# HGRN2 weights in blocks of 32 tokens: products on the four 32-column quarters of the array, and the level of 32 tokens as a product of its own

## The chip, the cores and the metric

The kernel runs on one core of a Trainium2 chip. A core has five engines that run side by side, each with its own stream of instructions: TensorE (PE, matrix products from SBUF into PSUM; a weight load, PEld, stands before every product), VectorE (DVE), ScalarE (ACT), GpSimd (POOL) and SyncE (SP, which starts transfers). They wait for one another by semaphores. The metric is the device time of one execution in microseconds (us).

## The reference, cut to what matters

Two layers over 256 tokens and a residual of width 2048. Each layer normalises the residual, projects it, runs two kinds of heads on the result (gated DeltaNet, 8 heads, and HGRN2, 8 heads, all of width 128), projects back, and adds a gated embedding. The change touches the HGRN2 heads alone, which compute

```
k = (1 - lb) * sigmoid(-f);  log_f = log(lb + (1 - lb) * sigmoid(f));  G = cumsum(log_f)
rel = masked_exp(causal, G[r] - G[s])           # for every channel d, for s <= r
A[r, s] = sum_d q[r, d] * k[s, d] * rel[r, s, d]
o[r] = (q[r] * exp(G[r])) @ S + sum_s A[r, s] * v[s]
```

`rel` differs from channel to channel, so A is not one plain product of a q matrix and a k matrix.

## The kernel before

The work of a layer is a long run of dense products (the projections "in", "out", "gate", "up"), all issued by `run_step`. Weights come from HBM in pieces (`load`, queued on SP), are split by ACT into `whi` (L398) and by DVE into the rest `wlo` (L400), and PE multiplies `whi`, `wlo` and the activations' two parts, 128x512 a time. PE's instructions stay in the order in which the program calls them (`PEOrder`, all at L334; transposes at L337). The other engines' instructions are put in order by the framework's scheduler.

The heads' work is laid between these products. Heads go in four groups of two (g = 0 to 3; `hg02` is layer 0, group 2; `dn02` the DeltaNet heads of that group). A group's mixer is a generator: after each `yield n` it goes on when n more steps of dense products have been issued (`tick`); the tables `DELAY` and `DELAY_AT` hold these n. So a mixer's small products stand in PE's order as short blocks between dense products.

The HGRN2 mixer is `HG.q_side`. Channels lie on the 128 partitions; the columns hold four pieces i (two heads x two chunks of 128 tokens). A is made by levels. At the level of unit u the tokens are taken in pairs of neighbouring runs of u tokens; s lies in the first run, r in the second, and with G's value at the end of the first run, `rel` is a factor of s times a factor of r. `factors(us)` builds for each u a tile X with k[s] exp(end - G[s]) in the first runs and q[r] exp(G[r] - end) in the second (DVE at L960, L962, L967, L974, exponentials on ACT at L965). `products` multiplies X by its own second runs:

```
for b in (0, 64):
    xb = x[:, i, b:b + 64]
    PE.matmul(pa[b:b + 64, c:c + 32], xb,
              xb.rearrange("p (n a b) -> p n a b", a=2, b=u)[:, :, 1], start=True, stop=True)
```

A product has 64 tokens as stationary columns and writes to PSUM partitions 0 to 63 or 64 to 127: one half of the array's columns. `place` copies the pairs that belong to the level by a mask `ms` from PSUM into `Ad` (128 x 4 x 64), on DVE, L991. Units 1 to 32 fill a block of 64 tokens; unit 64 and unit 128 are products of their own, copied by ACT. The level of single tokens and the diagonal share a product of 96 columns with `q8` (64 columns of q, 32 of q times a factor).

PE so has four blocks a group: first, the diagonal with level 1, then level 2 (bank "1"); second, levels 4 and 8; third, levels 16 and 32; fourth, levels 64 and 128. After the fourth, ACT copies `Ad`'s two halves into the block diagonal of `hA` (L1035), the 64 x 64 block (L1036) and `hAx`, and `po` multiplies them by v. With two layers and four groups there are eight such groups. A product of fp32 operands appears in the trace as two records, so that the program's x8 is x16 there; a product of two fp32r operands and a transpose are one.

Of the kernel before, what the change touches and what calls it, by code (L numbers as in the profile page):

```python
# [8 lines left out]
F32 = mybir.dt.float32  # L9
# [3 lines left out]
ALU = mybir.AluOpType  # L13
# [125 lines left out]


NPAR = _lay_params()
UNITS = (1, 2, 4, 8, 16, 32)


NMASK = 32 + 32 * len(UNITS)


def const_arrays():
    i = np.arange(128)
    c = np.zeros((128, 4 * 128 + 256 + 64), np.float32)  # L150
    c[:, 0:128] = np.eye(128)
    c[:, 128:256] = 1.0
    c[:, 256:384] = i[:, None] > i[None, :]
    c[:, 384:512] = i[:, None] <= i[None, :]
    c[:, 512:768] = (np.arange(256) % 128 != 0)[None, :]
    c[:, 768:832] = i[:, None] % 64 == np.arange(64)[None, :]
    s, r = i[:, None], i[None, :]
    m = np.zeros((128, NMASK), np.int32)
    m[:, 0:32] = (s % 64 // 32 == np.arange(32)[None, :] // 16) & (s % 32 < 16)
    for n, u in enumerate(UNITS):  # L160
        low = (s % 64 // (2 * u) == np.arange(32)[None, :] // u) & (s % (2 * u) < u)
        m[:, 32 + 32 * n:64 + 32 * n] = low
    return c, m


# [1 line left out]
def trunk(ctx: ExitStack, tc: tile.TileContext, head, xT, x, pT, W, par, fw, cst, msk, eye, out):  # L167
    nc = tc.nc
    pool = lambda name, bufs, **kw: ctx.enter_context(tc.tile_pool(name=name, bufs=bufs, **kw))
    cp = pool("const", 1)  # L170
# [10 lines left out]
    V, S, G = nc.vector, nc.scalar, nc.gpsimd  # L181
# [2 lines left out]

    h = [hp.tile([128, 2, 512], F32, name=f"h{c}") for c in range(4)]
    pr = cp.tile([128, NPAR], F32, name="pr")
    cs = cp.tile([128, 832], F32, name="cs")
    ms = cp.tile([128, NMASK], I32, name="ms")

    def first(out, in_):  # L190
# [77 lines left out]
        return [tuple(t) for t in a]  # L268

    ident, ones, SL, UI = (cs[:, 128 * j:128 * j + 128] for j in range(4))  # L270
    keep, ident64 = cs[:, 512:768], cs[:, 768:832]
    epsc = cp.tile([128, 1], F32, name="epsc")
    G.memset(epsc, EPS)
    lnhd = cp.tile([128, 1], F32, name="lnhd")
# [10 lines left out]
    hA = cp.tile([128, 4, 128], F32, name="hA")  # L285

    def clear_scratch():
        V.tensor_copy(SLr, SL)
        G.memset(hA[64:128, :, 0:64], 0.0)
        zero = tp.tile([128, 512], F32, tag="tmp", name="zero")  # L290
        G.memset(zero, 0.0)
        tc.keep_in_program_order(nc.scalar.dma_start(out=dfull(d2), in_=zero.rearrange("p (i c) -> p i c", i=4)))
# [8 lines left out]
    def bc1(ap, n):  # L301
        return ap.unsqueeze(1).to_broadcast([ap.shape[0], n, ap.shape[1]])
# [36 lines left out]
    PE = PEOrder()  # L339
# [222 lines left out]
    def mix(tag, n, bufs, name):  # L562
        return mp.tile([128, n], F32, tag=tag, name=name, bufs=bufs)
# [324 lines left out]
    class HG:  # L888
# [12 lines left out]
        def hi(self, ps, c0):  # L901
            self.v = mix("iv", 512, 2, self.n + "iv")
            for t in range(2):
                S.activation(self.v[:, 256 * t:256 * t + 256], ps[t][:, c0:c0 + 256], AF.Copy, scale=self.row.rt[:, t:t + 1])
            self.done.add("i")
            yield 1
# [24 lines left out]
        def q_side(self, qr):  # L931
            l, g, n = self.l, self.g, self.n

            q8 = mix("hq", 768, 1, n + "q").rearrange("p (a c) -> p a c", c=96)
            q = q8[:, :, 0:64]
            sg = tmp(n + "qsg")
            sigmoid(sg, qr)
            c64 = lambda ap: ap.rearrange("p (a c) -> p a c", c=64)
            V.tensor_tensor(q, c64(qr), c64(sg), ALU.mult)
            yield self.after("f")  # L940
            k, Gc = self.k, self.G
            k4 = v4(k)

            lo = lambda ap, u: ap.rearrange("p (n a b) -> p n a b", a=2, b=u)[:, :, 0]
            hi = lambda ap, u: ap.rearrange("p (n a b) -> p n a b", a=2, b=u)[:, :, 1]

            def hq(u):

                if u < 64:
                    return q.rearrange("p a (n c b) -> p a n c b", c=2, b=u)[:, :, :, 1]  # L950
                return q.rearrange("p (n c a) b -> p n c a b", c=2, a=u // 64)[:, :, 1]

            def factors(us):


                X = mix("hX", 1024, 2, n + f"X{us[0]}")[:, :512 * len(us)]
                xs = [X[:, 512 * j:512 * j + 512] for j in range(len(us))]
                for u, x in zip(us, xs):
                    ends = lo(Gc, u)[:, :, u - 1:u].to_broadcast([128, 256 // u, u])
                    V.tensor_tensor(lo(x, u), ends, lo(Gc, u), ALU.subtract)  # L960
                    if u < 128:
                        V.tensor_tensor(hi(x, u), hi(Gc, u), ends, ALU.subtract)  # L962
                    else:
                        V.tensor_copy(hi(x, u), hi(Gc, u))
                S.activation(X, X, AF.Exp)  # L965
                for u, x in zip(us, xs):
                    V.tensor_tensor(lo(x, u), lo(x, u), lo(k, u), ALU.mult)  # L967
                    hx = hi(x, u)
                    if u < 64:
                        hx = hx.rearrange("p (a n) b -> p a n b", a=8)  # L970
                    elif u == 128:
                        hx = hx.rearrange("p n (a b) -> p n a b", b=64)
                    hx_q = hq(u) if u != 64 else hq(u)[:, :, 0]
                    V.tensor_tensor(hx, hx, hx_q, ALU.mult)  # L974
                return [v4(x) for x in xs]

            def products(us, xs, pa, o=0):

                for j, (u, x) in enumerate(zip(us, xs)):
                    for i in range(4):  # L980
                        for b in (0, 64):
                            xb = x[:, i, b:b + 64]
                            c = o + 128 * j + 32 * i
                            PE.matmul(pa[b:b + 64, c:c + 32], xb,
                                      xb.rearrange("p (n a b) -> p n a b", a=2, b=u)[:, :, 1], start=True, stop=True)

            def place(us, ws):
                for u, w in zip(us, ws):
                    mo = 32 + 32 * UNITS.index(u)
                    mk = ms[:, mo:mo + 32].rearrange("p (n b) -> p n b", b=u)  # L990
                    V.copy_predicated(Ad.rearrange("p i (n a b) -> p i n a b", a=2, b=u)[:, :, :, 1],  # L991
                                      mk.unsqueeze(1).to_broadcast([128, 4, 32 // u, u]),
                                      w.rearrange("p i (n b) -> p i n b", b=u))

            bank = lambda x: pm.tile([128, 512], F32, tag="m", name=n + "pa" + x)
            v32 = lambda ap: ap.rearrange("p (i c) -> p i c", c=32)
            if self.wait("q"):
                yield self.wait("q")
            x1 = q8[:, :, 64:96]
            c32 = lambda ap: ap.rearrange("p (a n) b -> p a (n b)", a=8)  # L1000
            V.tensor_tensor(x1, c32(hi(Gc, 1)), c32(lo(Gc, 1)), ALU.subtract)
            S.activation(x1, x1, AF.Exp)
            V.tensor_tensor(x1, x1, hq(1)[:, :, :, 0], ALU.mult)
            xs = factors((2,))
            yield self.wait("a")

            Ad = mix("hAd", 256, 1, n + "Ad").rearrange("p (i c) -> p i c", i=4)
            pa = bank("1")
            for i in range(4):
                for b in (0, 64):  # L1010
                    PE.matmul(pa[b:b + 64, 96 * i:96 * i + 96], k4[:, i, b:b + 64], q8[:, 2 * i + b // 64, :],
                              start=True, stop=True)
            nxt = factors((4, 8))
            products((2,), xs, pa, 384)
            w1 = pa[:, :384].rearrange("p (i c) -> p i c", c=96)
            V.tensor_tensor(Ad, w1[:, :, 0:64], bc1(ident64, 4), ALU.mult)
            place((1, 2), (w1[:, :, 64:96], v32(pa[:, 384:512])))
            yield self.wait("u1")
            for us, then in (((4, 8), (16, 32)), ((16, 32), (64, 128))):
                xs, nxt = nxt, factors(then)  # L1020
                pa = bank(f"{us[0]}")
                products(us, xs, pa)
                place(us, (v32(pa[:, 0:128]), v32(pa[:, 128:256])))
                yield self.wait(f"u{us[0]}")
            xs = nxt
            pa = bank("64")
            for i in range(4):
                PE.matmul(pa[0:64, 64 * i:64 * i + 64], xs[0][:, i, 0:64], xs[0][:, i, 64:128], start=True, stop=True)

            for hh in range(2):  # L1030
                PE.matmul(pa[:, 256 + 128 * hh:384 + 128 * hh], xs[1][:, 2 * hh], xs[1][:, 2 * hh + 1],
                          start=True, stop=True)
            A = hA
            for b in (0, 64):
                S.copy(A[b:b + 64, :, b:b + 64], Ad[b:b + 64])  # L1035
            S.copy(A[0:64, :, 64:128], pa[0:64, :256].rearrange("p (a b) -> p a b", b=64))  # L1036
            Ax = v4(mix("hAx", 256, 1, n + "Ax"))
            S.copy(Ax, v4(pa)[:, 2:4])
# [153 lines left out]
    for l in range(DEPTH):  # L1192
# [24 lines left out]
        for c, k4 in order:  # L1217
# [6 lines left out]
            for q in range(0, 4, w):  # L1224
# [19 lines left out]
                s = run_step(ps[c], act)  # L1244
# [27 lines left out]
        for c, k4 in order:  # L1272
# [15 lines left out]
            if end and k4[3] == KT - 9:  # L1288

                n = state["next"]  # L1290
# [46 lines left out]
```

## Time and profile before

| | |
|---|---|
| median of the runs shown | 1275.14 us (three runs: 1274.43, 1275.14, and one of 6480.21) |
| profiled execution | 1273.78 us, of which 1272.1 us from the first to the last instruction |
| PE products, weight loads | 1259.3 us (99%), 1048.7 us (82%), 7297 records each |
| DVE, ACT, POOL busy | 926.7 us (73%), 782.6 us (62%), 64.4 us (5%) |
| granted TensorE clock | 0.998 |
| DMA | 220.87 MB, mean 174 GB/s |

PE's records overlap: a dense product lasts 0.39 us but the next starts 0.23 us after it. So for PE the distance from start to start is the cost, and the busy time only says that there is hardly a hole.

### The profile page before, as it was taken

What the parts mean: (1) busy time and instruction counts of PE and PEld (TensorE: products, weight loads), DVE (VectorE), ACT (ScalarE), POOL (GpSimd) and SP (SyncE); (2) the same over time, 40 slices, a digit from 0 to 9 for tenths busy, and PEclk for the clock granted to TensorE, in tenths of its full rate; (3) what the DMA queues carried; (4) which work ended last, traced back from release to release, by engine and by line L of the source; (5) the groups of instructions that cost most, each with busy time, mean ns of one, the idle gap of its engine ahead of it and who ended that gap; (6) DMA issues with size and microseconds to landing.
All of it is one profiled execution on the core that took longest, in us unless ns stands there. A gap on an engine that the chain in (4) does not pass through costs nothing.

```text
span 1272.1 us, 19685 instructions
## 1 busy us (share of the span) xinstructions
PE 1259.3 (99%) x7297; PEld 1048.7 (82%) x7297; DVE 926.7 (73%) x1744; ACT 782.6 (62%) x1395; POOL 64.4 (5%) x55
## 2 busy tenths in 40 slices
PE   9999999999999999999999999999999999999996
PEld 8988888888888888888888888888888888888886
DVE  7789689787796855547668886897777968555476
ACT  7666666666666654447557667667665766444464
POOL 0100010020000000000002000100100000000010
PEclk9999999999999999999999999999999999999999
DMA  8665545455554455555555555544555545555563
GB/s 286 192 229 159 172 159 165 131 166 178 167 167 153 144 174 182 183 189 191 184 185 169 176 163 159 170 141 135 178 182 170 162 150 171 182 182 185 183 198 132
DMA packets 78239, 220.87 MB, mean 174 GB/s; under 512 B 15552, under 2 KB 25280, under 8 KB 78144
## 3 DMA queue, kind: packets, MB, share of 16 engines
q1 hardware_dynamic: 59040, 211.73, 50.7%
q10 hardware_dynamic: 19104, 7.90, 2.3%
q8 instruction: 57, 0.93, 0.3%
q14 instruction: 38, 0.31, 0.1%
HBM read 214.88 MB, written 4.72 MB: 173 GB/s over the span
## 4 chain that ended last, share of the span: by engine, by line
PE 93%; DVE 5%; DMA 1%; issue 1%; ACT 1%; SPq 0%; DVEq 0%; ACTq 0%
PE out L334 14%; PE gate L334 13%; PE in1dk L334 7%; PE in0dk L334 7%; PE in1hf L334 6%; PE in0hf L334 6%; PE in0dv L334 6%; PE in1dv L334 6%; PE in0hi L334 5%; PE in1hi L334 5%; PE up L334 2%; DVE wlo L400 1%; PE in1dz L334 1%; PE in0dz L334 1%; PE gaterun L334 0%
## 5 line engine op out<-in xcount | busy, mean ns | idle before, releaser
L400 DVE TENSOR_TENSOR wlo<-raw,whi 128x1024 fp32r<-128x1024 f32 (+1 forms) x392 | 480.3, 1228 | 248.7 <-ACT whi L398 247.0
L398 ACT ACTIVATE whi<-raw 128x1024 fp32r<-128x1024 f32 (+1 forms) x392 | 411.4, 1051 | 352.1 <-PE out L334 88.3
L334 PE MATMUL in1hf<-whi,n1hi 128*128 128x512 f32 x128 | 52.5, 410 | 0.0
L334 PE MATMUL in1hi<-whi,n1hi 128*128 128x512 f32 x128 | 51.6, 403 | 0.0
L334 PE MATMUL in1dk<-whi,n1hi 128*128 128x512 f32 x128 | 51.2, 400 | 0.0
L334 PE MATMUL in1dk<-wlo,n1hi 128*128 128x512 f32 x128 | 50.0, 391 | 0.2 <-DVE wlo L400 0.2
L334 PE MATMUL gate<-whi,g0hi 128*128 128x512 f32 x128 | 50.2, 392 | 0.0
L334 PE MATMUL in1hf<-whi,n1lo 128*128 128x512 f32 x128 | 50.1, 391 | 0.0
L334 PE MATMUL in1hi<-whi,n1lo 128*128 128x512 f32 x128 | 50.0, 391 | 0.0
L334 PE MATMUL in1hf<-wlo,n1hi 128*128 128x512 f32 x128 | 49.9, 390 | 0.0
L334 PE MATMUL in1dk<-whi,n1lo 128*128 128x512 f32 x128 | 49.9, 390 | 0.0
L334 PE MATMUL in1hi<-wlo,n1hi 128*128 128x512 f32 x128 | 49.9, 390 | 0.0
L334 PE MATMUL gate<-whi,g0lo 128*128 128x512 f32 x128 | 49.8, 389 | 0.0
L334 PE MATMUL gate<-wlo,g0hi 128*128 128x512 f32 x128 | 49.8, 389 | 0.0
L334 PE MATMUL in1dv<-whi,n1hi 128*128 128x512 f32 (+1 forms) x128 | 48.3, 378 | 0.0
L334 PE MATMUL in1dv<-wlo,n1hi 128*128 128x512 f32 (+1 forms) x128 | 46.6, 364 | 0.0
L334 PE MATMUL in1dv<-whi,n1lo 128*128 128x512 f32 (+1 forms) x128 | 46.6, 364 | 0.0
L334 PE MATMUL gate<-whi,g1hi 128*128 128x512 f32 (+1 forms) x120 | 45.5, 379 | 0.0
L334 PE MATMUL gate<-wlo,g1hi 128*128 128x512 f32 (+1 forms) x120 | 45.4, 379 | 0.0
L334 PE MATMUL gate<-whi,g1lo 128*128 128x512 f32 (+1 forms) x120 | 45.4, 378 | 0.0
L334 PE MATMUL in0hf<-whi,n0hi 128*128 128x512 f32 x96 | 39.2, 408 | 0.0
L334 PE MATMUL in0hi<-whi,n0hi 128*128 128x512 f32 x96 | 38.5, 401 | 0.0
(1587 smaller groups left out, 3268.7 us busy)
## 6 DMA issues: line engine op xcount, KB each, us to landing
raw<-W SPq DMA_DIRECT2D x384, 512.0 KB, 3.5
raw<-W SPq DMA_DIRECT2D x7, 544.0 KB, 4.6
h<-x SPq DMA_DIRECT2D x4, 512.0 KB, 5.2
xt<-xT SPq DMA_DIRECT2D x3, 512.0 KB, 6.0
out_dram<-h SPq DMA_DIRECT2D x6, 256.0 KB, 2.2
fw<-fw ACTq DMA_DIRECT2D x2, 512.0 KB, 5.9
pin<-pT ACTq DMA_DIRECT2D x2, 256.0 KB, 3.2
out_dram<-h ACTq DMA_DIRECT2D x2, 256.0 KB, 3.0
```

The source lines that it names most:

```text
L334: return tc.keep_in_program_order(nc.tensor.matmul(*a, **k))
L398: S.activation(hi[:, sl], raw[:, sl], AF.Copy)
L400: V.tensor_tensor(lo[:, sl], raw[:, sl], hi[:, sl].bitcast(F32), ALU.subtract)
```

## The change

Blocks of 32 tokens take the place of blocks of 64. A product of levels 1 to 16 now has 32 stationary columns and writes 32 PSUM partitions, one of four quarters, with half as many moving columns (16 in place of 32, 48 in place of 96): twice as many products of a quarter of the size. `Ad`, the masks and `q8`'s pieces are half as wide. Level 32 leaves `products` and `place`: it is eight products of 32 x 32 into the same bank as level 16, and two DVE copies bring them straight into `hA`. Level 64 is eight products of 32 stationary columns in place of four of 64. ACT copies `Ad` into `hA` in four pieces of 32 partitions in place of two of 64, and two more blocks of `hA` are zeroed once at the start.

```diff
-UNITS = (1, 2, 4, 8, 16, 32)
+UNITS = (1, 2, 4, 8, 16)
...
-NMASK = 32 + 32 * len(UNITS)
+NMASK = 32 + 16 * len(UNITS)
...
     G.memset(hA[64:128, :, 0:64], 0.0)
+    for b in (0, 64):
+        G.memset(hA[b + 32:b + 64, :, b:b + 32], 0.0)
...
-q8 = mix("hq", 768, 1, n + "q").rearrange("p (a c) -> p a c", c=96)
-q = q8[:, :, 0:64]
+q8 = mix("hq", 768, 1, n + "q").rearrange("p (a c) -> p a c", c=48)
+q = q8[:, :, 0:32]
...
 def products(us, xs, pa, o=0):
     for j, (u, x) in enumerate(zip(us, xs)):
         for i in range(4):
-            for b in (0, 64):
-                xb = x[:, i, b:b + 64]
-                c = o + 128 * j + 32 * i
-                PE.matmul(pa[b:b + 64, c:c + 32], xb,
+            for b in range(0, 128, 32):
+                xb = x[:, i, b:b + 32]
+                c = o + 64 * j + 16 * i
+                PE.matmul(pa[b:b + 32, c:c + 16], xb,
                           xb.rearrange("p (n a b) -> p n a b", a=2, b=u)[:, :, 1], start=True, stop=True)
...
-Ad = mix("hAd", 256, 1, n + "Ad").rearrange("p (i c) -> p i c", i=4)
+Ad = mix("hAd", 128, 1, n + "Ad").rearrange("p (i c) -> p i c", i=4)
 pa = bank("1")
 for i in range(4):
-    for b in (0, 64):
-        PE.matmul(pa[b:b + 64, 96 * i:96 * i + 96], k4[:, i, b:b + 64], q8[:, 2 * i + b // 64, :],
+    for b in range(0, 128, 32):
+        PE.matmul(pa[b:b + 32, 48 * i:48 * i + 48], k4[:, i, b:b + 32], q8[:, 4 * i + b // 32, :],
                   start=True, stop=True)
...
-for us, then in (((4, 8), (16, 32)), ((16, 32), (64, 128))):
-    xs, nxt = nxt, factors(then)
-    pa = bank(f"{us[0]}")
-    products(us, xs, pa)
-    place(us, (v32(pa[:, 0:128]), v32(pa[:, 128:256])))
-    yield self.wait(f"u{us[0]}")
+xs, nxt = nxt, factors((16, 32))
+pa = bank("4")
+products((4, 8), xs, pa)
+place((4, 8), (v16(pa[:, 0:64]), v16(pa[:, 64:128])))
+yield self.wait("u4")
+A = hA
+xs, nxt = nxt, factors((64, 128))
+pa = bank("16")
+products((16,), xs, pa)
+for i in range(4):
+    for b in (0, 64):
+        PE.matmul(pa[b:b + 32, 64 + 32 * i:96 + 32 * i], xs[1][:, i, b:b + 32], xs[1][:, i, b + 32:b + 64],
+                  start=True, stop=True)
+place((16,), (v16(pa[:, 0:64]),))
+for b in (0, 64):
+    V.tensor_copy(A[b:b + 32, :, b + 32:b + 64], pa[b:b + 32, 64:192].rearrange("p (i c) -> p i c", c=32))
+yield self.wait("u16")
 xs = nxt
 pa = bank("64")
 for i in range(4):
-    PE.matmul(pa[0:64, 64 * i:64 * i + 64], xs[0][:, i, 0:64], xs[0][:, i, 64:128], start=True, stop=True)
+    for b in (0, 32):
+        PE.matmul(pa[b:b + 32, 64 * i:64 * i + 64], xs[0][:, i, b:b + 32], xs[0][:, i, 64:128],
+                  start=True, stop=True)
...
-for b in (0, 64):
-    S.copy(A[b:b + 64, :, b:b + 64], Ad[b:b + 64])
+for b in range(0, 128, 32):
+    S.copy(A[b:b + 32, :, b:b + 32], Ad[b:b + 32])
```

What moves in the engines' orders, at the three places of which the prediction speaks. First PE's first block of group hg00, between dense products of the key projection (`in0dk`). Columns: line, operation, output <- inputs (with buffer numbers), stationary x moving columns, count. Before:

```order
L334 MATMUL in0dk_1_1044<-wlo_1149,n0hi_313 128x512
L334 MATMUL in0dk_1_1044<-whi_1148,n0lo_314 128x512
L334 MATMUL hg00pa_1212<-hg00q,hg00k 64x96 x8
L334 MATMUL hg00pa_1212<-hg00X_1103 64x32 x8
L334 MATMUL in0dk_0_1043<-whi_1177,n0hi_392 128x512
```

and after:

```order
L336 MATMUL in0dk_1_1046<-wlo_1151,n0hi_313 128x512
L336 MATMUL in0dk_1_1046<-whi_1150,n0lo_314 128x512
L336 MATMUL hg00pa_1214<-hg00q,hg00k 32x48 x16
L336 MATMUL hg00pa_1214<-hg00X_1105 32x16 x16
L336 MATMUL in0dk_0_1045<-whi_1179,n0hi_392 128x512
```

The block stands at the same place, with twice the products. Second, PE's third block of group hg02, which follows a DeltaNet block of 32 x 32 products (`dn03px`). Before:

```order
L334 MATMUL in0hf_1_4167<-wlo_4218,n0hi_229 128x512
L334 MATMUL in0hf_1_4167<-whi_4217,n0lo_230 128x512
L334 MATMUL dn03px_4281<-dn03Tt,dn03P_4242 32x32 x8
L334 MATMUL hg02pa_4309<-hg02X_4186 64x32 x16
L334 MATMUL in0hf_0_4166<-whi_4247,n0hi_307 128x512
```

and after:

```order
L336 MATMUL in0hf_1_4279<-wlo_4346,n0hi_229 128x512
L336 MATMUL in0hf_1_4279<-whi_4345,n0lo_230 128x512
L336 MATMUL dn03px_4409<-dn03Tt,dn03P_4370 32x32 x8
L336 MATMUL hg02pa_4437<-hg02X_4298 32x16 x16
L336 MATMUL hg02pa_4437<-hg02X_4298 32x32 x8
L336 MATMUL in0hf_0_4278<-whi_4375,n0hi_307 128x512
```

Level 16 is 16 quarter products, level 32 eight products that use two of the four quarters. Third, DVE behind the third block of group hg01, where it also works on the query side of the DeltaNet group 2 (`dn02qac`, the convolution, and `dn02kq`, what the products `dn02pg` read). Before:

```order
L991 COPY_PREDICATED hg01Ad<-ms,hg01pa_2628 128x8x16
L662 SCALAR_TENSOR_TENSOR dn02qac<-dn02pqc,pr,dn02qac 128x254
L991 COPY_PREDICATED hg01Ad<-ms,hg01pa_2628 128x4x32
L662 SCALAR_TENSOR_TENSOR dn02qac<-dn02pqc,pr,dn02qac 128x253
L708 TENSOR_SCALAR b<-ssk 128x4
```

and after:

```order
L992 COPY_PREDICATED hg01Ad<-ms,hg01pa_2709 128x4x16
L664 SCALAR_TENSOR_TENSOR dn02qac<-dn02pqc,pr,dn02qac 128x254
L1035 COPY hA<-hg01pa_2709 32x4x32
L664 SCALAR_TENSOR_TENSOR dn02qac<-dn02pqc,pr,dn02qac 128x253
L1035 COPY hA<-hg01pa_2709 32x4x32
L710 TENSOR_SCALAR b<-ssk 128x4
```

One masked copy of level 32 is gone and two plain copies of 32 partitions stand in its place. Elsewhere on DVE a weight rest `wlo` changes places with a neighbour here and there; on ACT the four copies of `Ad` stand about where the two stood.

More of the change, by code (lines that the diff above doesn't have):

```diff
@@ L141 @@
 NPAR = _lay_params()
-UNITS = (1, 2, 4, 8, 16, 32)
-NMASK = 32 + 32 * len(UNITS)
+UNITS = (1, 2, 4, 8, 16)
+NMASK = 32 + 16 * len(UNITS)
 def const_arrays():
     i = np.arange(128)
-    c = np.zeros((128, 4 * 128 + 256 + 64), np.float32)
+    c = np.zeros((128, 4 * 128 + 256 + 32), np.float32)
     c[:, 0:128] = np.eye(128)
@@ L155, in const_arrays @@
     c[:, 512:768] = (np.arange(256) % 128 != 0)[None, :]
-    c[:, 768:832] = i[:, None] % 64 == np.arange(64)[None, :]
+    c[:, 768:800] = i[:, None] % 32 == np.arange(32)[None, :]
     s, r = i[:, None], i[None, :]
@@ L160, in const_arrays @@
     for n, u in enumerate(UNITS):
-        low = (s % 64 // (2 * u) == np.arange(32)[None, :] // u) & (s % (2 * u) < u)
-        m[:, 32 + 32 * n:64 + 32 * n] = low
+        low = (s % 32 // (2 * u) == np.arange(16)[None, :] // u) & (s % (2 * u) < u)
+        m[:, 32 + 16 * n:48 + 16 * n] = low
     return c, m
@@ L186, in trunk @@
     pr = cp.tile([128, NPAR], F32, name="pr")
-    cs = cp.tile([128, 832], F32, name="cs")
+    cs = cp.tile([128, 800], F32, name="cs")
     ms = cp.tile([128, NMASK], I32, name="ms")
@@ L270, in trunk @@
     ident, ones, SL, UI = (cs[:, 128 * j:128 * j + 128] for j in range(4))
-    keep, ident64 = cs[:, 512:768], cs[:, 768:832]
+    keep, ident32 = cs[:, 512:768], cs[:, 768:800]
     epsc = cp.tile([128, 1], F32, name="epsc")
@@ L932, in q_side @@
             l, g, n = self.l, self.g, self.n
-            q8 = mix("hq", 768, 1, n + "q").rearrange("p (a c) -> p a c", c=96)
-            q = q8[:, :, 0:64]
+            q8 = mix("hq", 768, 1, n + "q").rearrange("p (a c) -> p a c", c=48)
+            q = q8[:, :, 0:32]
             sg = tmp(n + "qsg")
             sigmoid(sg, qr)
-            c64 = lambda ap: ap.rearrange("p (a c) -> p a c", c=64)
-            V.tensor_tensor(q, c64(qr), c64(sg), ALU.mult)
+            c32 = lambda ap: ap.rearrange("p (a c) -> p a c", c=32)
+            V.tensor_tensor(q, c32(qr), c32(sg), ALU.mult)
             yield self.after("f")
@@ L947, in hq @@
             def hq(u):
-                if u < 64:
+                if u < 32:
                     return q.rearrange("p a (n c b) -> p a n c b", c=2, b=u)[:, :, :, 1]
-                return q.rearrange("p (n c a) b -> p n c a b", c=2, a=u // 64)[:, :, 1]
+                return q.rearrange("p (n c a) b -> p n c a b", c=2, a=u // 32)[:, :, 1]
             def factors(us):
@@ L968, in factors @@
                     hx = hi(x, u)
[L969 to L974, printed above, removed]
+                    if u < 32:
+                        hx = hx.rearrange("p (a n) b -> p a n b", a=16)
+                    elif u > 32:
+                        hx = hx.rearrange("p n (a b) -> p n a b", b=32)
+                    V.tensor_tensor(hx, hx, hq(u) if u != 32 else hq(u)[:, :, 0], ALU.mult)
                 return [v4(x) for x in xs]
@@ L988, in place @@
                 for u, w in zip(us, ws):
-                    mo = 32 + 32 * UNITS.index(u)
-                    mk = ms[:, mo:mo + 32].rearrange("p (n b) -> p n b", b=u)
+                    mo = 32 + 16 * UNITS.index(u)
+                    mk = ms[:, mo:mo + 16].rearrange("p (n b) -> p n b", b=u)
                     V.copy_predicated(Ad.rearrange("p i (n a b) -> p i n a b", a=2, b=u)[:, :, :, 1],
-                                      mk.unsqueeze(1).to_broadcast([128, 4, 32 // u, u]),
+                                      mk.unsqueeze(1).to_broadcast([128, 4, 16 // u, u]),
                                       w.rearrange("p i (n b) -> p i n b", b=u))
             bank = lambda x: pm.tile([128, 512], F32, tag="m", name=n + "pa" + x)
-            v32 = lambda ap: ap.rearrange("p (i c) -> p i c", c=32)
+            v16 = lambda ap: ap.rearrange("p (i c) -> p i c", c=16)
             if self.wait("q"):
                 yield self.wait("q")
-            x1 = q8[:, :, 64:96]
-            c32 = lambda ap: ap.rearrange("p (a n) b -> p a (n b)", a=8)
-            V.tensor_tensor(x1, c32(hi(Gc, 1)), c32(lo(Gc, 1)), ALU.subtract)
+            x1 = q8[:, :, 32:48]
+            odd = lambda ap: ap.rearrange("p (a n) b -> p a (n b)", a=16)
+            V.tensor_tensor(x1, odd(hi(Gc, 1)), odd(lo(Gc, 1)), ALU.subtract)
             S.activation(x1, x1, AF.Exp)
@@ L1005, in q_side @@
             yield self.wait("a")
-            Ad = mix("hAd", 256, 1, n + "Ad").rearrange("p (i c) -> p i c", i=4)
+            Ad = mix("hAd", 128, 1, n + "Ad").rearrange("p (i c) -> p i c", i=4)
             pa = bank("1")
             for i in range(4):
-                for b in (0, 64):
-                    PE.matmul(pa[b:b + 64, 96 * i:96 * i + 96], k4[:, i, b:b + 64], q8[:, 2 * i + b // 64, :],
+                for b in range(0, 128, 32):
+                    PE.matmul(pa[b:b + 32, 48 * i:48 * i + 48], k4[:, i, b:b + 32], q8[:, 4 * i + b // 32, :],
                               start=True, stop=True)
             nxt = factors((4, 8))
[L1014 to L1017, printed above, removed]
+            products((2,), xs, pa, 192)
+            w1 = pa[:, :192].rearrange("p (i c) -> p i c", c=48)
+            V.tensor_tensor(Ad, w1[:, :, 0:32], bc1(ident32, 4), ALU.mult)
+            place((1, 2), (w1[:, :, 32:48], v16(pa[:, 192:256])))
             yield self.wait("u1")
-            for us, then in (((4, 8), (16, 32)), ((16, 32), (64, 128))):
-                xs, nxt = nxt, factors(then)
-                pa = bank(f"{us[0]}")
-                products(us, xs, pa)
-                place(us, (v32(pa[:, 0:128]), v32(pa[:, 128:256])))
-                yield self.wait(f"u{us[0]}")
+            xs, nxt = nxt, factors((16, 32))
[15 more added lines that the diff above has]
+            yield self.wait("u16")
             xs = nxt
@@ L1032, in q_side @@
                           start=True, stop=True)
-            A = hA
-            for b in (0, 64):
-                S.copy(A[b:b + 64, :, b:b + 64], Ad[b:b + 64])
+            for b in range(0, 128, 32):
+                S.copy(A[b:b + 32, :, b:b + 32], Ad[b:b + 32])
             S.copy(A[0:64, :, 64:128], pa[0:64, :256].rearrange("p (a b) -> p a b", b=64))
```

## The prediction

> **What bounds the kernel now.** I read the page's busy times first, then its chain, then PE's waits.
>
> ```profile
> span 1272.1 us, 19685 instructions
> ...
> PE 1259.3 (99%) x7297; PEld 1048.7 (82%) x7297; DVE 926.7 (73%) x1744; ACT 782.6 (62%) x1395; POOL 64.4 (5%) x55
> ...
> PE 93%; DVE 5%; DMA 1%; issue 1%; ACT 1%; SPq 0%; DVEq 0%; ACTq 0%
> ```
>
> The last line gives the engines' shares of the chain that ended last: PE carries 93% of it. Who PE waited for, from the chain of waits of PE alone (in total, times, longest):
>
> ```profile
> PE warm L334 <- DVE zeros L237: 1.1, 1, 1.1
> PE in0dz L334 <- DVE wlo L400: 0.9, 1, 0.9
> PE in0dk L334 <- DVE wlo L400: 0.2, 1, 0.2
> PE in1dk L334 <- DVE wlo L400: 0.2, 1, 0.2
> ```
>
> That is 2.4 us in all. PE is full; a microsecond taken out of its stream is a microsecond off the end, as long as DVE and ACT bring the operands that much earlier. So what counts is the distance from start to start in PE's blocks, and the timeline shows it. First block of group hg00 (start, length, engine, line, operation, count of records):
>
> ```profile
> 98.64 0.39 PE L334 MATMUL in0dk<-wlo,n0hi 128*128 128x512 f32 x1
> 98.87 0.39 PE L334 MATMUL in0dk<-whi,n0lo 128*128 128x512 f32 x1
> 99.18 0.88 PE L334 MATMUL hg00pa<-hg00q,hg00k 128*64 128x96 f32 x16
> 99.89 0.61 PE L334 MATMUL hg00pa<-hg00X 128*64 128x32 f32 x16
> 100.43 0.50 PE L334 MATMUL in0dk<-whi,n0hi 128*128 128x512 f32 x1
> 100.77 0.39 PE L334 MATMUL in0dk<-wlo,n0hi 128*128 128x512 f32 x1
> ```
>
> A dense product costs 0.23 us (98.64 to 98.87). Entering the block costs 0.08 more (98.87 to 99.18 is 0.31), and the second dense product behind it starts 0.34 after the first. The change touches neither. The block itself takes 1.25 us from 99.18 to 100.43: 0.71 for diagonal and level 1, 0.54 for level 2. The second block of that group, and a stretch in group hg02 where a DeltaNet block of 32 x 32 products stands right before the third block:
>
> ```profile
> 108.82 1.12 PE L334 MATMUL hg00pa<-hg00X 128*64 128x32 f32 x32
> 109.87 0.66 PE L337 MATMUL dn01pkc<-cs,dn01kqet 128*128 128x128 f32 x4
> ...
> 393.57 0.39 PE L334 MATMUL in0hf<-whi,n0lo 128*128 128x512 f32 x1
> 393.88 0.44 PE L334 MATMUL dn03px<-dn03Tt,dn03P 32*32 32x32 f32 x16
> 394.25 1.12 PE L334 MATMUL hg02pa<-hg02X 128*64 128x32 f32 x32
> 395.31 0.50 PE L334 MATMUL in0hf<-whi,n0hi 128*128 128x512 f32 x1
> ```
>
> and how long one record of each kind lasts (min/median/max in ns):
>
> ```profile
> L334 PE MATMUL dn01pp<-dn01T,dn01Bt x16: 191/191/212, 206.1 to 206.4; 32*32 32x32 f32 x16
> L334 PE MATMUL hg02pa<-hg02X x92: 192/223/377, 374.1 to 405.6; 128*64 128x32 f32 x80, 128*64 128x64 f32 x8, 128*128 128x128 f32 x4
> ```
>
> A run of records is as long as its starts plus the last record. So 32 records of 64 stationary columns start over 1.12 - 0.22 = 0.90 us, 58 ns for a turn of the two halves. The 16 records of 32 columns start over 0.44 - 0.19 = 0.25 us: 31 ns for a turn of two tiles, about 16 ns a record. Length goes with the stationary columns, and two tiles side by side cost one turn. The way out is 394.25 - 394.13 = 0.12 after 32-column tiles and 395.31 - 395.15 = 0.16 after halves (0.15 at 109.87); I count 0.03 less.
>
> **PE's blocks, if four quarters go abreast as two tiles do.** A turn of four quarters then costs 31 ns; a turn with 48 moving columns I take at half of 0.71/8 = 89 ns, 44 ns.
> First block: 8 x 0.044 + 8 x 0.031 + 0.12 = 0.72 in place of 1.25: -0.53.
> Second: 16 x 0.031 + 0.12 = 0.62 in place of 1.05: -0.43.
> Third: eight turns for level 16, eight turns of two quarters for level 32, 0.62 in place of 1.06: -0.44.
> Fourth:
>
> ```profile
> 130.52 1.32 PE L334 MATMUL hg00pa<-hg00X 128*64 128x64 f32 x12
> 131.67 0.81 PE L334 MATMUL dn01pg<-dn01kq 128*128 128x256 f32 x3
> ```
>
> Level 64 had four products, each alone, with 64 moving columns; it now has eight, two abreast, with the same 64 moving columns. I leave its turns as they are and take only the way out, -0.03.
> Sum -1.43 a group, times eight groups **-11.4 us**. This is the one bound.
>
> **Can PE be fed so fast?** Twice the products mean 64 records in the first and the second block and 48 in the third, where there were 32 each. At 31 ns for four, a record comes every 8 ns. The trace has no such rate. Its closest records are those 16 at 16 ns, and they are only 16 in a row; the densest 48 in a row are those from 393.88 to 395.31, 30 ns each, ways out included. So the feed lies between no limit and 30 ns for every record beyond the first 16, which I take as standing ready when the block begins.
> At 30 ns: first block 48 x 0.030 + 0.12 = 1.56 (+0.31), second the same (+0.51), third 32 x 0.030 + 0.12 = 1.08 (+0.02), fourth -0.03; +0.81 a group, **+6.5 us**. This is the other bound.
> I take the nearest row, 16 ns: 48 x 0.016 + 0.12 = 0.89 (-0.36 and -0.16), 32 x 0.016 + 0.12 = 0.63 (-0.43), -0.03; -0.98 a group, **-7.8 us**.
>
> [...]
>
> **DVE and ACT.** Prices before, for hg01 and a 32-partition copy:
>
> ```profile
> L991 DVE COPY_PREDICATED hg01Ad<-ms,hg01pa x6: 288/294/446, 211.5 to 234.7; 128x128 f32<-128x128 int32 x6
> L1016 DVE TENSOR_TENSOR hg01Ad<-hg01pa,cs x1: 425/425/425, 208.7 to 208.7; 128x256 f32<-128x256 f32 x1
> L1035 ACT COPY hA<-hg01Ad x2: 390/397/404, 236.1 to 238.7; 64x256 f32<-64x256 f32 x2
> L804 ACT COPY dn01Tt<-dn01px x2: 255/256/258, 214.7 to 214.9; 32x128 f32<-32x128 f32 x2
> ```
>
> DVE: five masked copies at half the width save between nothing and half (0 to 0.74); at about 1 ns an element (128 elements in 0.29, 256 in 0.43) I take 64 x 5 = 0.32. The sixth goes, 0.29. The diagonal at 128 elements costs about 0.29 in place of 0.43, saving 0.13. Two copies of 32 x 128 out of PSUM are new; DVE shows none, and ACT's 0.26 and the masked copy's 0.29 bracket them: +0.55. Sum -0.2 us a group, between +0.15 and -0.6. The new copies wait for the bank that the masked copy ahead of them awaits, so nothing new is queued behind a wait. ACT: four copies at 0.26 less two at 0.40, +0.24 a group, 1.9 us over a kernel in which ACT idles 38%. The splits of q and of level 1 keep their elements; the tables loaded at the start shrink; the two clearings are on POOL, 5% busy. All these I set at nothing; without that cover they would cost at most the 1.9 us.
>
> **What is late next.** There is one place where PE already stands for DVE: the products `dn02pg`, behind hg01's third block.
>
> ```profile
> 239.59 0.61 PE L334 MATMUL dn01pS<-dn01v,dn01kt 128*128 128x128 f32 x4
> 239.76 0.76 DVE L670 TENSOR_TENSOR dn02kq<-dn02qac,dn02qsg 128x256 f32<-128x256 f32 x2 [0.38 <-ACT dn02qsg L469]
> 240.31 0.94 PEld L334 LDWEIGHTS dn02pg<-dn02kq 128*128 128x128 f32 x5 [0.31 <-PE dn01pS L334]
> 240.34 1.10 PE L334 MATMUL dn02pg<-dn02kq 128*128 128x256 f32 x4
> ```
>
> The weight load idled 0.31 us until DVE had `dn02kq`. From the blocks to there DVE is nearly full:
>
> ```profile
> 205.00:240.00 35.00, 35.00 (x282) 28.32 (x280) 31.63 (x74) 23.62 (x45) 0.00 (x0) 1.00 0.47 152
> ```
>
> 31.63 of 35 us (the fourth number). PE comes 0.36 + 0.16 + 0.43 = 0.95 us sooner, DVE only its 0.2: 0.75 goes into that wait, in both layers: **+1.5 us**. Bounds: nothing, if all of DVE's chain moves with PE, and all of the 0.95, 1.9 us. Of the other waits the two of 0.2 us for `wlo` may grow by as little.
>
> **Sum.** The profiled execution took 1273.78 us, the span 1272.1 and 1.7 around it; it lies 0.1% under the median of 1275.14 and I make the sum against it: 1273.8 - 7.8 + 1.5 = **1267.5 us**.
>
> **Rivals.**
> A: quarters without any limit of feed. For it: nothing in the trace shows a limit, the 16 records at 16 ns keep an even beat. Against: 8 ns a record is not seen. -11.4, and 1.2 a layer lost at `dn02pg`: -9.0, 1264.8 us.
> B, slower: the stream of PE's instructions is the bound inside the blocks. The place is the first and second block, the price 30 ns a record beyond 16: 1280.3 us, and no wait is added at `dn02pg`. It decides from 3.03/128 = 24 ns a record on: 3.36 us for the three old blocks less three ways out at 0.12 and with 0.03 of the fourth, over the 128 records beyond the ready ones. For it: 48 records in a row never came closer than 30 ns. Against: those were held back by 64-column loads.
> [...]
> C: the change doesn't do what it says, quarters go two abreast only. A turn of four is then two turns, 62 ns (89 with 48 columns): 1.33, 1.11 and 0.86 us for the blocks, -0.09 a group, 1273 us. For it: no row with four tiles. Against: two halves and two 32-tiles both run side by side.
> D: PE's gain is as forecast but more of DVE's work sits in the way than at `dn02pg`, and half of it is lost: 1270 us. Against: 346 us of DVE's 1272 are idle.
>
> **How the numbers follow.** Forecast 0.33, A 0.27, B 0.20, C 0.12, D 0.08. The range goes from A with little lost, 1263, into B, 1281, and leaves out the far ends of both. 2% of this kernel is 25 us, about what a measurement can tell from no change; no case reaches it: same 0.97, faster 0.01, slower 0.02.
>
> **What would show it.** In the timeline after: `hg00pa` with x16, x16, x32 become x32, x32, x64. First block 0.9 us from its start to the next dense product and second block 0.9 say the forecast; 0.7 and 0.6 say A; 1.6 say B; 1.3 and 1.1 say C. The third block should be 0.6 in both A and the forecast. The idle time before `dn02pg` should grow from 0.3 to about 1.1. PE's share of the chain stays over 90%. The forecast is wrong if PE's waits grow by several microseconds, or if a turn of four quarters depends on something that two tiles don't show.

## The result and the profile after

The changed kernel takes 1264.12 us (median of six runs, 1263.59 to 1265.59) against 1274.79 us for the kernel before on the same chip: a ratio of 0.9922, 95% interval 0.9912 to 0.9933. The profiled execution took 1263.90 us in place of 1273.78. One of the six executions before took 6480.21 us; the ratio is taken without it. The gain of 0.8% is clear of noise and inside the 2% that I called no change. The forecast was 1267.5 in a range from 1263 to 1281, so the time stands near the lower end; the rival A, four quarters abreast without a limit of feed, stood at 1264.8.

From the page after: the span, the engines, the chain by engine.

```profile
span 1262.1 us, 21116 instructions
...
PE 1248.5 (99%) x8001; PEld 1036.7 (82%) x8001; DVE 923.6 (73%) x1752; ACT 785.1 (62%) x1411; POOL 65.2 (5%) x57
...
PE 92%; DVE 5%; ACT 1%; issue 1%; DMA 0%; SPq 0%; ACTq 0%; DVEq 0%
```

PE issues 704 products and 704 weight loads more and is done 10 us sooner. It is still the bound, with 92% of the chain. The blocks in PE's timeline (start, length, operation, count of records): the first block of hg00 and of hg01, the second of hg00, the third of hg02, the fourth of hg00, each with what follows it.

```profile
99.04 0.55 PE L336 MATMUL hg00pa<-hg00q,hg00k 128*32 128x48 f32 x32
99.54 0.45 PE L336 MATMUL hg00pa<-hg00X 128*32 128x16 f32 x32
99.91 0.50 PE L336 MATMUL in0dk<-whi,n0hi 128*128 128x512 f32 x1
...
205.19 0.55 PE L336 MATMUL hg01pa<-hg01q,hg01k 128*32 128x48 f32 x32
205.55 0.47 PE L336 MATMUL hg01pa<-hg01X 128*32 128x16 f32 x32
205.95 0.50 PE L336 MATMUL in0dk<-whi,n0hi 128*128 128x512 f32 x1
...
108.30 0.74 PE L336 MATMUL hg00pa<-hg00X 128*32 128x16 f32 x64
108.96 0.66 PE L339 MATMUL dn01pkc<-cs,dn01kqet 128*128 128x128 f32 x4
...
391.10 0.71 PE L336 MATMUL hg02pa<-hg02X 128*32 128x16 f32 x48
391.74 0.50 PE L336 MATMUL in0hf<-whi,n0hi 128*128 128x512 f32 x1
...
129.26 1.28 PE L336 MATMUL hg00pa<-hg00X 128*32 128x64 f32 x20
130.38 0.60 PE L336 MATMUL dn01pg<-dn01kq 128*128 128x256 f32 x2
```

From a block's start to the next product: first block 0.76 us (205.19 to 205.95) in place of 1.25, second 0.66 in place of 1.05, third 0.64 in place of 1.06, fourth 1.12 in place of 1.15. That is 1.33 us a group. In hg00 and its twin of layer 1 the first block is 0.87 and 0.85, because level 2 begins 0.50 and 0.48 us after the diagonal there and 0.36 elsewhere. So PE's blocks are 10.4 us shorter in all. What PE waits for now (the 1.1 us for `zeros` at the start stays as it was):

```profile
PE in0dz L336 <- ACT whi L263: 0.7, 1, 0.7
PE dn12pg L336 <- DVE dn12kq L672: 0.5, 1, 0.5
PE dn02pg L336 <- DVE dn02kq L672: 0.5, 1, 0.5
PE in0dz L336 <- DVE wlo L402: 0.5, 1, 0.5
PE in0dk L336 <- DVE wlo L402: 0.2, 1, 0.2
PE in1dk L336 <- DVE wlo L402: 0.2, 1, 0.2
```

The 0.7 us for `whi` is new, but it stands at 7.6 us, long before the first HGRN2 block, where other runs of this case have between 0 and 1.0 us. The wait at `dn02pg` grew, as the prediction had it, but by less, and the experiments show that the reason was another one.

### The profile page after: what moved, and what is told of

The parts are those of the page before. It is cut to its first block, busy times and chain, and to the rows that moved or that the text cites. A ratio compares the mean times of both kernels' runs of the same rounds, so it can differ in the third digit from the quotient of the medians.

```text
span 1262.1 us, 21116 instructions
## 1 busy us (share of the span) xinstructions
PE 1248.5 (99%) x8001; PEld 1036.7 (82%) x8001; DVE 923.6 (73%) x1752; ACT 785.1 (62%) x1411; POOL 65.2 (5%) x57
## 4 chain that ended last, share of the span: by engine, by line
PE 92%; DVE 5%; ACT 1%; issue 1%; DMA 0%; SPq 0%; ACTq 0%; DVEq 0%
PE out L336 14%; PE gate L336 13%; PE in1dk L336 7%; PE in0dk L336 7%; PE in1hf L336 6%; PE in0hf L336 6%; PE in0dv L336 6%; PE in1dv L336 6%; PE in1hi L336 5%; PE in0hi L336 5%; PE up L336 2%; DVE wlo L402 1%; PE in1dz L336 1%; PE in0dz L336 1%; ACT whi L400 1%
```

## The experiments

**1. How fast can PE be fed?** The forecast and the rival A differ in this alone. The second block's products, four times over:

```diff
-products((4, 8), xs, pa)
+for _ in range(4):
+    products((4, 8), xs, pa)
```

> The second block's products (levels 4 and 8) are issued four times over, 256 records in place of 64. Theory S (what the trace after suggests: each quarter takes its own records in order, 32 ns each, and PE's stream brings at least one record every 8.3 ns, the beat at the end of that block): the block's starts grow from 0.55 to 0.55 + 192 x 0.0083 = 2.15 us, +12.8 us over eight groups, about 1277 us. Theory F (the prediction's: records beyond those that stand ready come every 16 ns, and more of them stood ready than I took): 0.55 + 192 x 0.016 = 3.6 us, +24.6 us, about 1288 us.

It took 1309.46 us (one execution), more than either theory. The timeline of PE in the second block of hg00; in brackets the idle time and what ended it:

```profile
108.14 2.19 PE L336 MATMUL hg00pa<-hg00X 128*32 128x16 f32 x239
113.90 0.42 PE L336 MATMUL hg00pa<-hg00X 128*32 128x16 f32 x17 [3.58 <-issue]
```

The first 239 records start over 2.19 - 0.18 = 2.0 us, 8.4 ns each: theory F's 16 ns is dead. Then PE stands for 3.58 us, and "issue" means that it waits for nothing that the profile shows. Every one of the eight blocks has one such stop, 0.6 to 3.7 us, 18.8 us in PE's waits. Behind this one the granted clock was 0.50 from 114 to 117 us; behind the stops of 0.6 and 0.9 us it stayed at 1.00, behind the other six it fell. Over the whole run it was 0.987 in place of 0.997, and 1% of 1308 us is about the rest of the 45 us (12.8 for the records, 18.8 for the stops). What PE stops for shows in the DMA queue that brings its instructions, in the page's table, first of the changed kernel, then of this run:

```profile
q8 instruction: 63, 1.03, 0.3%
```

```profile
q8 instruction: 75, 1.23, 0.4%
```

Twelve more pieces of 16.4 KB for 1536 products and as many loads more: 256 instructions a piece, 128 records with their loads. The block eats a piece in 1.1 us. Between 110.4 and 113.8 us, inside the stop, the table has one piece:

```profile
q8 instruction: 1, 0.02, 1.7%
```

It lands at 112.43 us and PE goes on at 113.90. In all eight blocks PE goes on 1.3 to 1.6 us after a piece has landed, and every stop comes between the 137th and the 241st record, in the second half of the block. That fits a queue in which the piece that begins in the first 128 records is there in time and the next is not.

So the same, twice:

```diff
-products((4, 8), xs, pa)
+for _ in range(2):
+    products((4, 8), xs, pa)
```

> The second block's products are issued twice, 128 records in place of 64. With four times each block had one stop of 0.6 to 3.8 us that waited for nothing but PE's instructions, and the whole run fetched 12 pieces of instructions more for 3072 more instructions (256 a piece, so 128 records with their weight loads). Theory P (one piece ahead is there, the second isn't): 128 records need at most one new piece, no stop: second block 0.55 + 64 x 0.0083 = 1.09 us, +4.3 us, 1268.4 us. Theory Q (any piece that begins inside a dense block stops PE): stops in several of the eight blocks, 1272 us or more.

1269.61 us (one execution), and the second block of hg01:

```profile
216.29 1.27 PE L336 MATMUL hg01pa<-hg01X 128*32 128x16 f32 x128
217.49 0.50 PE L336 MATMUL in0dv<-whi,n0ahi 128*128 128x512 f32 x1
```

1.20 us with its way out, all eight blocks alike, no stop: theory P. The changed kernel's blocks of 64 records are well inside what PE takes without a stop. The beat in the long run, 8.5 ns a record (1.27 - 0.18 = 1.09 us for 128), is a little over the 7.8 ns of a turn of 31 ns by four, and so the second block is 0.66 and not the 0.62 of rival A. As four quarters can hardly take records faster, these runs bound the feed and don't measure it.

**2. Do the four quarters run abreast, and does the order matter?** The same products, within each level one quarter after the other, eight records each:

```diff
-for i in range(4):
-    for b in range(0, 128, 32):
+for b in range(0, 128, 32):
+    for i in range(4):
```

> The same products, but all of one quarter one after the other and then the next quarter's (diagonal, levels 1 to 16). If a record waits for the record ahead of it in the stream (theory S with starts in the order of the stream): one record per turn, first block 32 x 0.043 + 32 x 0.032 = 2.4 us in place of 0.65, second 64 x 0.032 = 2.0 in place of 0.55, third 1.3 in place of 0.51: +4.0 us a group, +32 us, about 1296 us. If PE looks ahead over the 8 to 16 records of one quarter: blocks as they are, 1264 us.

1279.12 us (one execution), between the two. PE's first and second block of hg01:

```profile
207.18 1.00 PE L336 MATMUL hg01pa<-hg01q,hg01k 128*32 128x48 f32 x29
207.98 0.20 PE L336 MATMUL hg01pa<-hg01X 128*32 128x16 f32 x1
208.02 0.21 PE L336 MATMUL hg01pa<-hg01q,hg01k 128*32 128x48 f32 x1
208.03 0.18 PE L336 MATMUL hg01pa<-hg01X 128*32 128x16 f32 x1
208.06 0.21 PE L336 MATMUL hg01pa<-hg01q,hg01k 128*32 128x48 f32 x1
...
217.76 1.50 PE L336 MATMUL hg01pa<-hg01X 128*32 128x16 f32 x64
219.19 0.50 PE L336 MATMUL in0dv<-whi,n0ahi 128*128 128x512 f32 x1
```

The second block now starts over 1.50 - 0.18 = 1.32 us, 41 turns of 32 ns in place of 64 one by one or 16 four abreast. So neither theory holds as it stood: PE neither waits strictly for the record ahead nor sees all the quarters' work. And the rows of the first block show records of level 2 starting at 207.98 and 208.03, before the diagonal records at 208.02 and 208.06, though the program has all the diagonal's first. So records that use another quarter start ahead of those that stand before them in the program, over some stretch of the stream shorter than what it takes here to fill four quarters; how long that stretch is was not measured. Of the two orders that were run, four abreast came only with the quarters alternating.

**3. Is it the stationary columns or the moving ones?** Levels 2 to 16 with 64 stationary and 16 moving columns; half of these levels' weights are left out.

```diff
-for b in range(0, 128, 32):
-    xb = x[:, i, b:b + 32]
-    PE.matmul(pa[b:b + 32, c:c + 16], xb, ...
+for b in (0, 64):
+    PE.matmul(pa[b:b + 64, c:c + 16], x[:, i, b:b + 64], ...
```

> Levels 2 to 16 with 64 stationary columns again, but only 16 moving columns: half as many products, and half of these levels' weights are left out. If a turn is set by the stationary columns: 58 ns a turn as before, second block 0.90 us in place of 0.55, level 2 and level 16 0.46 in place of 0.25 each, +0.8 us a group, +6.2 us, about 1270 us. If the moving columns set it: turns of 32 ns or less, second block at most 0.5 us, about 1263 us or less.

1273.41 us (one execution). The second block of hg01:

```profile
217.59 1.11 PE L336 MATMUL hg01pa<-hg01X 128*64 128x16 f32 x32
218.64 0.50 PE L336 MATMUL in0dv<-whi,n0ahi 128*128 128x512 f32 x1
```

1.05 us by these rows, as the block of before with 32 moving columns. Fewer moving columns give next to nothing in levels 2 to 16; the gain there is from 32 stationary columns with four tiles abreast. The diagonal, where 96 moving columns became 48, was not taken apart in this way. (The whole came out 3 us over the expectation. 1.5 us of it is in PE's blocks, where the way from 64-column to 32-column tiles within a block costs about 0.1 us more than I took; two waits of 0.5 us for `wlo` came beside that.)

**4. Is DVE's work covered?** The two copies of level 32, three times:

```diff
-for b in (0, 64):
+for b in (0, 64, 0, 64, 0, 64):
     V.tensor_copy(A[b:b + 32, :, b + 32:b + 64], ...
```

> The two DVE copies of level 32 are done three times, 4 more of 0.28 us a group, 9 us of DVE in all. If DVE is beside the path but for dn02pg (the prediction): only that wait can grow, by up to 1.1 us a layer, 1264 to 1266 us. If DVE's work carries through to the end: up to 1273 us.

1267.96 us, ratio to before 0.9949 (0.9933 to 0.9966), so 3.8 us more than the changed kernel. PE's waits:

```profile
PE in0dv L336 <- DVE wlo L402: 1.3, 1, 1.3
PE in1dv L336 <- DVE wlo L402: 1.3, 1, 1.3
PE dn02pg L336 <- DVE dn02kq L672: 1.1, 1, 1.1
PE dn12pg L336 <- DVE dn12kq L672: 1.1, 1, 1.1
```

The expectation is wrong by a second place: behind hg00's third block the copies stand in DVE's queue ahead of a `wlo`, and PE waits 1.3 us for it in each layer. Of 9 us of added DVE work 3.8 came through, in two of a layer's four groups.

**5. What lengthened the wait at dn02pg?** I had said that PE comes sooner and DVE doesn't. The rows tell otherwise. After the change, the load that waits:

```profile
238.08 1.59 PEld L336 LDWEIGHTS dn02pg<-dn02kq 128*128 128x128 f32 x8 [0.64 <-PE dn01pS L336]
```

The row names PE's `dn01pS`, but the load starts 0.12 us after the end of the first `dn02kq`, before and after alike, while `dn01pS` ended 0.45 us ahead of it after the change: it waits for DVE. PE's first product behind hg01's third block, and the first `dn02kq` on DVE. Before (the row of `dn02kq`, at 239.76, stands in the prediction), and after:

```profile
233.61 0.44 PE L337 MATMUL dn02ssk<-cs,dn02kq 128*128 128x128 f32 x2
```

```profile
231.02 0.68 PE L339 MATMUL dn02ssk<-cs,dn02kq 128*128 128x128 f32 x4
...
237.54 0.76 DVE L672 TENSOR_TENSOR dn02kq<-dn02qac,dn02qsg 128x256 f32<-128x256 f32 x2 [0.27 <-ACT dn02qsg L471]
```

and, after, the groups of hg01's copies (min/median/max in ns):

```profile
L1048 ACT COPY hA<-hg01Ad x4: 281/294/298, 232.8 to 236.6; 32x128 f32<-32x128 f32 x4
L992 DVE COPY_PREDICATED hg01Ad<-ms,hg01pa x5: 215/218/292, 210.1 to 231.9; 128x64 f32<-128x64 int32 x5
L1035 DVE COPY hA<-hg01pa x2: 269/279/289, 232.4 to 233.1; 32x128 f32<-32x128 f32 x2
L1017 DVE TENSOR_TENSOR hg01Ad<-hg01pa,cs x1: 290/290/290, 207.4 to 207.4; 128x128 f32<-128x128 f32 x1
```

From the block's end to `dn02kq` it is 239.76 - 233.61 = 6.15 us before and 237.54 - 231.02 = 6.52 after. In experiments 2 and 3, where PE's first three blocks of hg01 are 2.0 and 1.0 us longer than after, it is 241.42 - 234.92 = 6.50 and 240.83 - 234.33 = 6.50. So in these four runs the stretch hangs on PE's own block and follows it; it became 0.37 us longer by itself. DVE waits at its end for ACT's `dn02qsg`, and ACT has four copies of 0.29 there in place of two of 0.40: 0.38 us. The test, those four copies on GpSimd:

```diff
-S.copy(A[b:b + 32, :, b:b + 32], Ad[b:b + 32])
+G.tensor_copy(A[b:b + 32, :, b:b + 32], Ad[b:b + 32])
```

> The four copies of Ad into hA go from ACT to GpSimd. From the way out of hg01's third block to the end of the first dn02kq it took 6.58 us before and 6.94 after, and 6.92 and 6.93 in the two runs with longer blocks. If ACT's copies (1.17 us in place of 0.79) are what lengthened it: 6.94 - 1.17 = 5.8 us or as far as DVE's own work lets it, PE's 0.65 us ahead of dn02pg and dn12pg go, about 1262.8 us. If DVE's two copies of level 32 did it: 6.9 us stays, 1264 us.

1262.94 us, ratio to before 0.9912 (0.9898 to 0.9927). PE's timeline and DVE's:

```profile
231.63 0.44 PE L339 MATMUL dn02ssk<-cs,dn02kq 128*128 128x128 f32 x2
...
237.40 0.42 DVE L672 TENSOR_TENSOR dn02kq<-dn02qac,dn02qsg 128x256 f32<-128x256 f32 x1
...
238.08 0.60 PE L336 MATMUL dn02pg<-dn02kq 128*128 128x256 f32 x2
```

5.77 us from start to start, 0.75 less than after the change, and PE's waits no longer name `dn02kq`. (The expectation counted to the end of the first `dn02kq`; by that measure it is 6.19, so the whole 1.17 us did not come. DVE now goes straight from a `wlo` to `dn02kq`, without waiting for ACT.) Calling these products a step of 2.8 us later does the same by other means:

```diff
-"d2D": 9, "d2k": 3,
+"d2D": 9, "d2q": 6, "d2F": 2, "d2k": 3,
```

> The products dn02pg and dn12pg, for which PE stands 0.65 us each after the change, are called one step of dense products later (2.8 us). If the wait is theirs alone: 1.3 us less than the changed kernel, about 1262.8 us. If DVE as a whole is late there, PE waits for a wlo instead: 1264 us.

1262.46 us, 0.9908 (0.9895 to 0.9922). Both intervals reach into that of the changed kernel, so the 1.2 and 1.7 us are likely and not certain by the times alone; that the waits are gone is in the traces.

**6. What is left to take.** Levels 32 and 64 use two of the four quarters. Here the odd pieces go to the other two:

```diff
-PE.matmul(pa[b:b + 32, 64 + 32 * i:96 + 32 * i], xs[1][:, i, b:b + 32], ...
+h, c = b + 32 * (i % 2), 64 + 32 * (i // 2)
+PE.matmul(pa[h:h + 32, c:c + 32], xs[1][:, i, b:b + 32], ...
 ...
-PE.matmul(pa[b:b + 32, 64 * i:64 * i + 64], xs[0][:, i, b:b + 32], ...
+h, c = b + 64 * (i % 2), 64 * (i // 2)
+PE.matmul(pa[h:h + 32, c:c + 64], xs[0][:, i, b:b + 32], ...
```

> Levels 32 and 64 of the odd pieces go to the two quarters that the even pieces leave empty: four abreast in place of two. If a turn costs the same with four as with two: third block 0.51 to 0.38 us (four turns of 32 ns less), fourth 0.22 us less (four turns of 56 ns), 0.35 us a group, 2.8 us in all: 1261.3 us, and up to 1 us more where the two added DVE copies and the added ACT copy fall into the chain ahead of dn02pg. If two of the quarters can't run beside the other two with these widths: 1264 us or more.

1263.20 us, 0.9913 (0.9900 to 0.9927). PE's third block of hg02 runs to 0.55 us (391.43 to 391.98) from 0.64 and the fourth of hg00 to 0.90 (129.94 to 130.84) from 1.12, 0.30 us in most groups; the third blocks of hg01 and hg11 keep their 0.63. That is 2.2 us in all, but only 0.9 arrive, and as the intervals overlap even these are likely and not certain. The waits say where the rest went:

```profile
PE in0dv L336 <- DVE wlo L402: 0.6, 1, 0.6
PE in1dv L336 <- DVE wlo L402: 0.6, 1, 0.6
```

It is the place of experiment 4, behind hg00's third block, reached with two DVE copies more. Then the cost of going into tiles and out:

```diff
-"h0a": 5, "h0yp": 2,
-"h1f": 2, "h1u4": 4, "h1yp": 3,
-"h2a": 5, "h2o": 1, "h2yp": 2,
+"h0a": 5, "h0yp": 2, "h0u4": 2, "h0u16": 4,
+"h1f": 2, "h1u1": 2, "h1u4": 3, "h1u16": 5, "h1yp": 3,
+"h2a": 5, "h2u1": 4, "h2u4": 2, "h2u16": 2, "h2o": 2, "h2yp": 2,
```

> Five blocks a layer (third of hg00, second and third of hg01, second and fourth of hg02) are moved by one or two steps so that they stand right behind a DeltaNet block of 32- or 64-column products. If entering and leaving tiles costs by the block, each saves 0.17 us on the way in (0.32 to 0.15) and 0.11 us at the second dense product behind it, 2.8 us in all: 1261.3 us. If the operands aren't ready at the earlier places (DVE is 92% busy around hg01): waits of PE of 0.5 us and more there, 1264 us or more.

1267.88 us, 0.9955 (0.9941 to 0.9969), slower than the changed kernel by 3.8 us. The way in is cheaper as expected, 0.15 or 0.12 us in place of 0.32. But moving the blocks also changes the order of DVE's and ACT's work: `dn02kq` now stands behind a `wlo` that itself waits for ACT's `whi`, and starts at 239.40 us in place of 237.54. Which of the five moves did this was not tested. The wait, and PE around it by stretches, then PE behind the same wait in layer 1 (the last three numbers are the granted clock, the DMA share and GB/s):

```profile
PE dn02pg L336 <- DVE dn02kq L672: 2.9, 1, 2.9
```

```profile
237.00:240.00 3.00, 0.12 (x2) 0.06 (x1) 2.16 (x4) 2.01 (x4) 0.00 (x0) 1.00 0.56 177
240.00:243.00 3.00, 3.00 (x9) 2.39 (x9) 1.10 (x4) 0.00 (x0) 0.00 (x0) 0.53 0.55 176
...
868.00:871.00 3.00, 3.00 (x17) 2.53 (x16) 0.89 (x4) 0.29 (x1) 0.64 (x1) 1.00 0.40 131
```

Each layer has a hole of 2.9 us. Behind that of layer 0 the clock was 0.53 over 3 us, about half as much again lost; behind that of layer 1 it was 1.00. Level 32 and 64 spread, the moved blocks and the later `dn02pg` together:

> The three together. If they are independent: 1.3 + 2.8 + 2.8 us less than the changed kernel, about 1257 us. If DVE sets the end of what is won: 1260 us or more.

1261.09 us, 0.9895 (0.9881 to 0.9908): `dn02pg` a step later takes away the hole, and 1.1 and 1.8 us of waits for a `wlo` at `in0hi` and `in1hi` appear in its place. With level 32 as in the changed kernel, the copies of Ad on GpSimd and hg01's blocks left where they were:

> Level 64 on four quarters, dn02pg one step later, the copies of Ad on GpSimd, and the blocks of groups 0 and 2 alone moved next to a DeltaNet block. PE's stream: 8 x 0.21 + 6 x 0.28 = 3.4 us shorter, waits 1.3 us shorter: 1259.4 us if DVE keeps up, 1261 us if the wlo that stood in the way in v3 stays late.

1262.43 us, 0.9907 (0.9890 to 0.9923). And with level 32 spread too, its odd copies on ACT:

```diff
-for b in (0, 64):
-    V.tensor_copy(A[b:b + 32, :, b + 32:b + 64], ...
+for m, copy in enumerate((V.tensor_copy, S.copy)):
+    for b in (0, 64):
+        copy(A[b:b + 32, m::2, b + 32:b + 64], pa[b + 32 * m:b + 32 * m + 32, 64:128] ...
```

> As v4, and level 32 on four quarters with the odd pieces' copies on ACT: the third block 0.09 us shorter (0.51 to 0.42 in v1), 0.7 us in all, no work added on DVE: 1258.7 us if DVE keeps up. If ACT's added 0.5 us a group is in a chain: as v4 or slower.

1260.43 us, 0.9893 (0.9879 to 0.9908). This one and the three edits together, whose 0.9895 can't be told from it, are the fastest, and both intervals lie just below the changed kernel's. In these last two runs the `wlo` at `in0hi` and `in1hi` stays late, 1.0 to 1.1 us a layer, so of the 4.7 us expected of the first 1.7 came, and of the second's 5.4, 3.7. Why the second gains 2 us over the first with only 0.7 us less in PE's blocks was not settled; the profile of the first has waits of 0.8 us for `dn00kqet` and 0.6 for `hg12fqet`, ACT's evictions, that the other lacks.

## Why the prediction was right or wrong

- **What bounds the kernel**: right. PE carries 92% of the chain, and of 10.4 us taken from its blocks 9.9 came off the profiled execution.
- **Four quarters in a turn of two**: right, and the sum of -11.4 us was 1 us too large. The blocks measured 0.76, 0.66, 0.64 and 1.12 where it had 0.72, 0.62, 0.62 and 1.12; hg00's first block lost 0.1 more a layer.
- **The feed, 16 ns for each record beyond the first 16**: the step that failed, and the main reason, 2.6 of 3.4 us, why the forecast stood too high. The feed in the long run was no slower than 8.4 ns a record, so it did not set the 16 ns of those 16 records. They were two tiles abreast, at 31 ns a turn of two. I had read that turn from the same row, and a row that is full for one reason can't price another. With the measured blocks the term is -10.4 in place of -7.8, and the sum 1264.9 with the +1.5 left in. Within one quarter the records come about 32 ns apart (31 to 32 in the first half of hg00's second block after); adding products on different tiles one by one was what failed.
- **B, the stream of instructions as the bound**: wrong in price and place for this kernel, real further out. The price isn't by the record, it is a stop of 0.6 to 3.7 us when a block of 256 records wants its second piece; 128 records had none. The first two blocks, at 0.76 and 0.66 us, are what the prediction's own signs gave to A (0.7 and 0.6), and not to the forecast (0.9 and 0.9). That A's 1264.8 is so near is in part luck: its blocks are 1 us too short and its wait 1.7 us too long.
- **C**, two abreast only, is out by the timeline. That the order of the quarters counts was not in the prediction at all. **D**, half of PE's gain lost on DVE, is out too: 9.9 of 10.4 us arrived.
- **The wait at `dn02pg`, +1.5 us**: the place was right, the size and the reason weren't. The idle time ahead of its weight load went from 0.31 to 0.64 us, in layer 1 from 0.30 to 0.65, +0.7 in both. The step by which PE comes 0.95 us sooner and DVE only its 0.2 failed: the stretch in front hangs on PE's block and moves with it. The growth was ACT's two added copies, which I had set at nothing because ACT idles 38%.
- **DVE's bill, -0.2 us a group**: right. Five masked copies of 0.22 in place of 0.29, the sixth gone, the diagonal 0.29 in place of 0.43, two copies of 0.28 new: -0.23. That it costs nothing held for this size only; experiment 4 found two places a layer where more of it reaches PE.

Both errors of size point the same way: 2.6 us too little gain in the blocks and 0.8 us too much loss at the wait make the 3.4. Against the profiled execution, 1263.90, the forecast is 3.6 us too high; the small remainder was not traced.

## What to carry to other kernels

Here small products packed by their stationary columns: four of 32, one on each quarter, cost one turn of about 32 ns when the program alternated the quarters, and halving the moving columns alone bought next to nothing (a second block of 1.05 us, as before). Before a rate is taken from a trace as a limit, ask what held that row back. And an engine that idles a third of the time still has stretches in which its next instruction is the one that the bound engine waits for: price an added copy by what stands behind it in the queue.

## What the runs showed of the hardware

PE took a weight load and a product every 8.4 ns, up to 239 pairs in a row, and then stopped, 0.6 to 3.7 us in the eight blocks, until 1.3 to 1.6 us after its next 256 instructions had landed. Records of one quarter started ahead of records of another that stand before them in the program (207.98 us ahead of 208.02 in experiment 2), by a limited stretch: with one quarter after the other the second block took 1.43 us (217.76 to 219.19), alternating 0.66. After a hole of 2.9 us PE ran at a granted clock of 0.53 for 3 us; after an equal one it ran at 1.00.
